# One 64 KB-row load for the first tile, weights issued after the table load, and a first token made by VectorE alone

## The chip, the core and the metric

The kernel runs on one core of one Trainium2 chip. The core has five engines with a queue of instructions each. Here three do the work: ScalarE (ACT) and VectorE (DVE) compute, SyncE (SP) only issues transfers; ACT's queue issues some transfers too. Transfers between the chip's large memory (HBM) and the on-chip memory (SBUF, 128 partitions) are carried out by 16 DMA engines, which all queues share. The metric is the device time of one execution in microseconds (us); a lower one is better.

## The reference

For each of 16 x 1024 = 16,384 tokens two expert outputs of 512 numbers are weighted and added, all in float32:

```python
batch, seq, hidden, n_experts, k = 16, 1024, 512, 8, 2
expert_outputs = randn(batch, seq, k, hidden)     # 67.1 MB
combine_weights = randn(batch, seq, k)            # 0.13 MB
out = np.sum(expert_outputs * combine_weights[..., np.newaxis], axis=2)   # 33.6 MB
```

## The kernel before, in words

**Tiles.** The 16,384 tokens are spread over 128 partitions, 128 tokens to a partition. A tile `et` holds `J` = 16 tokens of every partition: 128 rows of 16 x 1024 x 4 bytes = 64 KB, 8 MB in all. There are 8 tiles (loop on line 79, `g` = 0 to 7) and three buffers for them (`bufs=3`, line 47), so the load of tile `g` + 3 needs the store of tile `g` to be done. The text calls them load 0 to 7 and store 0 to 7.

**Weights.** All weights lie in one tile `wt`. Line 51 loads it in two transfers on ACT's queue: 112 KB (896 bytes to a partition) for tiles 0 to 6, and 16 KB (128 bytes to a partition) for tile 7.

**Warm-up.** Line 56 runs one tiny Copy on ACT, so that the loading of the function table that Copy needs comes early. In the order of ACT's queue it follows the two weight loads.

**Compute** (`combine`, lines 58 to 76). Per token ACT multiplies the first half of its 1024 numbers by the first weight, in place (line 65). DVE then computes the second half times the second weight plus ACT's result (line 68) and writes it to the front of the same tile, so a piece of `c` tokens is stored from `c` x 2 KB per partition.

**Loads and stores.** Loads are issued by SP (line 89). Tile 0 is loaded in two pieces: 2 tokens, cut into 4 KB rows by `max_dma_last_dim`, then 14 tokens in 56 KB rows; tiles 1 to 6 in one piece each with 64 KB rows; tile 7 in two pieces of 12 and 4 tokens (48 KB and 16 KB rows), each of which is computed and stored by itself. Stores of tiles 0 to 6 are issued by ACT's queue as one piece with 32 KB rows, those of tile 7 by SP in 24 KB and 8 KB rows (line 96). In the profile q1 is SP's DMA queue and q10 is ACT's: loads and the last two stores are in q1, weights and stores 0 to 6 in q10.

**What sets the order.** Each queue issues in the order of the program. SP issues loads 0, 1 and 2 at once, and each later load when the store that frees its buffer has landed. ACT issues a store when DVE has finished its tile.

Of the kernel before, what the change touches and what calls it, by code (L numbers as in the profile page):

```python
# [1 line left out]

# [4 lines left out]


@with_exitstack
def kernel(  # L10
    ctx: ExitStack,
    tc: tile.TileContext,
    expert_outputs: bass.AP,
    combine_weights: bass.AP,
    out: bass.AP,
):
    nc = tc.nc
    b, s, k, h = expert_outputs.shape
    assert k == 2
    n = b * s  # L20
    P = nc.NUM_PARTITIONS
    per = n // P
    assert per * P == n

    J = 16
    PIECES = (12, 4)
    assert sum(PIECES) == J and per % J == 0
    main = per - J
    eo = expert_outputs.rearrange("b s k h -> (b s) (k h)")
    cw = combine_weights.rearrange("b s k -> (b s) k")  # L30
    o = out.rearrange("b s h -> (b s) h")

    def rows(x):

        a = x[0 : P * main, :].rearrange("(p t) f -> p t f", p=P)
        b = x[P * main : n, :].rearrange("(p t) f -> p t f", p=P)
        return lambda t, c: a[:, t : t + c, :] if t < main else b[:, t - main : t - main + c, :]

    eo, cw, o = rows(eo), rows(cw), rows(o)

    dt = mybir.dt.float32
    mult = mybir.AluOpType.mult
    add = mybir.AluOpType.add
    copy = mybir.ActivationFunctionType.Copy

    wpool = ctx.enter_context(tc.tile_pool(name="w", bufs=1))
    ipool = ctx.enter_context(tc.tile_pool(name="in", bufs=3))

    wt = wpool.tile([P, per * k], dt)
    for t, c in ((0, main), (main, J)):  # L50
        nc.scalar.dma_start(
            out=wt[:, k * t : k * (t + c)].rearrange("p (t k) -> p t k", k=k), in_=cw(t, c)
        )

    warm = wpool.tile([P, 1], dt)
    nc.scalar.activation(out=warm, in_=nc.const_aps.tensor(1.0, (P, 1), dt), func=copy)  # L56

    def combine(et, a, c, t0):

        ot = et[:, a : a + c].rearrange("p j f -> p (j f)")[:, 0 : c * h]  # L60
        ot = ot.rearrange("p (j f) -> p j f", f=h)
        for i in range(c):
            t = t0 + a + i
            x = et[:, a + i]
            nc.scalar.activation(  # L65
                out=x[:, 0:h], in_=x[:, 0:h], func=copy, scale=wt[:, 2 * t : 2 * t + 1]
            )
            nc.vector.scalar_tensor_tensor(  # L68
                out=ot[:, i, :],
                in0=x[:, h : 2 * h],  # L70
                scalar=wt[:, 2 * t + 1 : 2 * t + 2],
                in1=x[:, 0:h],
                op0=mult,
                op1=add,
            )
        return ot

    last = per // J - 1
    for g in range(last + 1):
        et = ipool.tile([P, J, k * h], dt)  # L80
        t0 = g * J
        if g == 0:
            loads, stores = ((0, 2), (2, J - 2)), ((0, J),)
        elif g < last:
            loads = stores = ((0, J),)
        else:
            loads = stores = ((0, PIECES[0]), (PIECES[0], PIECES[1]))
        for a, c in loads:
            nc.sync.dma_start(  # L89
                out=et[:, a : a + c],  # L90
                in_=eo(t0 + a, c),
                max_dma_last_dim=k * h * 4 if t0 + a == 0 else None,
            )
        for a, c in stores:
            ot = combine(et, a, c, t0)
            (nc.sync if g == last else nc.scalar).dma_start(out=o(t0 + a, c), in_=ot)


# [1 line left out]
_INS = ['expert_outputs', 'combine_weights']  # L100
_OUTS = [((16, 1024, 512), 'float32')]


# [23 lines left out]
```

## Time and profile before

| what | value |
|---|---|
| median of 3 runs | 241.98 us (240.82 to 242.04) |
| the profiled execution | 242.21 us, of which the span from first to last instruction 240.4 us |
| busy: DVE, ACT | 87.2 us (36%), 81.0 us (34%) |
| moved by DMA | 100.82 MB, mean 419 GB/s over the span |
| one token: ACT line 65, DVE line 68 | 0.708 us, 0.746 us |
| table load, warm-up (line 56) | 1.283 us, 0.203 us |
| ACT waits for loads | 149.6 us in all, 10 times |
| SP waits for stores to free a buffer | 158.7 us in all, 5 times |

Issue and landing (the time at which the transfer's completion is seen) of some transfers, in us from the start of the span:

| transfer | issued | landed |
|---|---|---|
| tile 0, 2 tokens | 0.73 | 6.3 |
| weights, 112 KB | 0.73 | 5.4 |
| weights, 16 KB | 1.20 | 23.3 |
| tile 0, 14 tokens | 1.22 | 23.3 |
| load 1 | 1.73 | 47.72 |
| store 0 | 33.52 | 67.47 |
| load 3 | 67.55 | 106.69 |
| store 1 | 59.61 | 96.42 |
| load 7, 12 tokens | 183.86 | 217.85 |
| load 7, 4 tokens | 184.24 | 229.72 |
| store 6 | 205.62 | 226.91 |
| store 7, 12 tokens | 227.13 | 237.00 |
| store 7, 4 tokens | 233.65 | 239.42 |

How to read the profile: the page gives, among others, the busy share of the DMA engines in 40 equal slices of the span (tenths, 9 is 90% or more) and the chain of work that ended last, followed back from the last instruction. The timeline lists merged instructions with start, duration, engine, line and, in brackets, how long the engine stood idle before and for whom. The table of stretches gives for a stretch its length, the busy time of DVE, ACT and POOL, a clock, and the DMA engines' mean busy share and GB/s; packets are counted in the stretch in which they start. The DMA view gives the packets, MB and share of each queue in a window. A packet is one row of a transfer, or the 4-byte write of its completion on one of the 16 engines.

### The profile page before, as it was taken

What the parts mean: (1) busy time and instruction counts of PE and PEld (TensorE: products, weight loads), DVE (VectorE), ACT (ScalarE), POOL (GpSimd) and SP (SyncE); (2) the same over time, 40 slices, a digit from 0 to 9 for tenths busy, and PEclk for the clock granted to TensorE, in tenths of its full rate; (3) what the DMA queues carried; (4) which work ended last, traced back from release to release, by engine and by line L of the source; (5) the groups of instructions that cost most, each with busy time, mean ns of one, the idle gap of its engine ahead of it and who ended that gap; (6) DMA issues with size and microseconds to landing.
All of it is one profiled execution on the core that took longest, in us unless ns stands there. A gap on an engine that the chain in (4) does not pass through costs nothing.

```text
span 240.4 us, 412 instructions
## 1 busy us (share of the span) xinstructions
DVE 87.2 (36%) x128; ACT 81.0 (34%) x130; POOL 0.2 (0%) x4
## 2 busy tenths in 40 slices
DVE  0200950089001970019700295004930069205740
ACT  2201930095002940029400492005900078007440
POOL 0000000000000000000000000000000000000000
DMA  9989989899999999898999999999989999999895
GB/s 346 421 363 461 512 360 393 371 502 393 436 414 458 414 503 436 382 480 383 431 436 403 469 398 436 431 425 447 480 387 436 447 431 436 433 428 414 341 401 236
DMA packets 3155, 100.82 MB, mean 419 GB/s; under 512 B 464, under 2 KB 592, under 8 KB 848
## 3 DMA queue, kind: packets, MB, share of 16 engines
q1 hardware_dynamic: 1856, 71.30, 69.4%
q10 hardware_dynamic: 1296, 29.49, 28.5%
q14 instruction: 3, 0.02, 0.0%
HBM read 67.24 MB, written 33.55 MB: 419 GB/s over the span
## 4 chain that ended last, share of the span: by engine, by line
DMA 85%; DVE 6%; ACT 4%; issue 1%; SPq 1%; DVEq 0%; ACTq 0%
DMA et<-in_expert_outputs_dram 54%; DMA out_dram<-et 30%; DVE et L68 6%; ACT et L65 4%; SPq L89 1%; DVEq L122 0%; DVEq L68 0%; ACTq L65 0%
## 5 line engine op out<-in xcount | busy, mean ns | idle before, releaser
L68 DVE SCALAR_TENSOR_TENSOR et<-et,wt 128x512 f32<-128x512 f32 x128 | 87.2, 746 | 146.4 <-ACT et L65 144.6
L65 ACT ACTIVATE et<-et,wt 128x512 f32<-128x512 f32 x128 | 79.5, 708 | 149.6 <-DMA et<-in_expert_outputs_dram 149.6
L56 ACT ACT_TABLE_LOAD x1 | 1.3, 1283 | 1.7 <-issue 1.7
L56 ACT ACTIVATE warm<-const-float32-1.0 128x1 f32<-128x1 f32 x1 | 0.2, 203 | 0.0
L111 POOL MEMSET const-bfloat16-1.0<- 128x1 bf16 x1 | 0.1, 101 | 0.0
L111 POOL MEMSET const-uint8-127<- 128x1 uint8 x1 | 0.1, 101 | 0.0
L111 POOL MEMSET const-float32-0.0<- 128x1 f32 x1 | 0.1, 98 | 0.2 <-issue 0.2
L111 POOL MEMSET const-float32-1.0<- 128x1 f32 x1 | 0.1, 98 | 0.0
## 6 DMA issues: line engine op xcount, KB each, us to landing
out_dram<-et ACTq DMA_DIRECT2D x7, 4096.0 KB, 36.2
et<-in_expert_outputs_dram SPq DMA_DIRECT2D x1, 7168.0 KB, 22.1
et<-in_expert_outputs_dram SPq DMA_DIRECT2D x1, 6144.0 KB, 34.0
out_dram<-et SPq DMA_DIRECT2D x1, 3072.0 KB, 9.9
et<-in_expert_outputs_dram SPq DMA_DIRECT2D x1, 2048.0 KB, 45.5
et<-in_expert_outputs_dram SPq DMA_DIRECT2D x1, 1024.0 KB, 5.6
out_dram<-et SPq DMA_DIRECT2D x1, 1024.0 KB, 5.8
wt<-in_combine_weights_dram ACTq DMA_DIRECT2D x1, 112.0 KB, 4.6
```

Of the source, the lines that this page charges most:

```text
L56: nc.scalar.activation(out=warm, in_=nc.const_aps.tensor(1.0, (P, 1), dt), func=copy)
L65: nc.scalar.activation(out=x[:, 0:h], in_=x[:, 0:h], func=copy, scale=wt[:, 2 * t : 2 * t + 1])
L68: nc.vector.scalar_tensor_tensor(out=ot[:, i, :], in0=x[:, h : 2 * h], scalar=wt[:, 2 * t + 1 : 2 * t + 2], in1=x[:, 0:h], op0=mult, op1=add,)
L89: nc.sync.dma_start(out=et[:, a : a + c], in_=eo(t0 + a, c), max_dma_last_dim=k * h * 4 if t0 + a == 0 else None,)
L111: nc = _bacc.Bacc("TRN2", target_bir_lowering=False, num_devices=1)
```

## The change

Three things are changed. The order on ACT's queue: the warm-up, and with it the table load, goes first, and `issue_after` keeps the two weight loads behind it in the queue's order (an order within one engine, without a semaphore). The first token of every piece: DVE makes both products, the first with an added `tensor_scalar`, and ACT starts with the second token; a piece is 16 tokens, and 12 and 4 in tile 7. The loads: tile 0 comes in one transfer of 16 tokens in 64 KB rows like the others; tile 7 is as it was.

```diff
     wt = wpool.tile([P, per * k], dt)
-    for t, c in ((0, main), (main, J)):
-        nc.scalar.dma_start(
-            out=wt[:, k * t : k * (t + c)].rearrange("p (t k) -> p t k", k=k), in_=cw(t, c)
-        )
-
     warm = wpool.tile([P, 1], dt)
-    nc.scalar.activation(out=warm, in_=nc.const_aps.tensor(1.0, (P, 1), dt), func=copy)
+    table = nc.scalar.activation(out=warm, in_=nc.const_aps.tensor(1.0, (P, 1), dt), func=copy)
+    with tc.issue_after(table.ins):
+        for t, c in ((0, main), (main, J)):
+            nc.scalar.dma_start(
+                out=wt[:, k * t : k * (t + c)].rearrange("p (t k) -> p t k", k=k), in_=cw(t, c)
+            )
...
-            nc.scalar.activation(
-                out=x[:, 0:h], in_=x[:, 0:h], func=copy, scale=wt[:, 2 * t : 2 * t + 1]
-            )
+            w0 = wt[:, 2 * t : 2 * t + 1]
+            if i == 0:
+
+                nc.vector.tensor_scalar(
+                    out=x[:, 0:h], in0=x[:, 0:h], scalar1=w0, scalar2=None, op0=mult
+                )
+            else:
+                nc.scalar.activation(out=x[:, 0:h], in_=x[:, 0:h], func=copy, scale=w0)
...
-        if g == 0:
-            loads, stores = ((0, 2), (2, J - 2)), ((0, J),)
-        elif g < last:
-            loads = stores = ((0, J),)
-        else:
-            loads = stores = ((0, PIECES[0]), (PIECES[0], PIECES[1]))
-        for a, c in loads:
-            nc.sync.dma_start(
-                out=et[:, a : a + c],
-                in_=eo(t0 + a, c),
-                max_dma_last_dim=k * h * 4 if t0 + a == 0 else None,
-            )
-        for a, c in stores:
+        pieces = ((0, J),) if g < last else ((0, PIECES[0]), (PIECES[0], PIECES[1]))
+        for a, c in pieces:
+            nc.sync.dma_start(out=et[:, a : a + c], in_=eo(t0 + a, c))
+        for a, c in pieces:
             ot = combine(et, a, c, t0)
```

## The prediction

> **What bounds the kernel now.** I read the chain of waits first, then the DMA line of the page, then the same stretch by stretch.
>
> ```profile
> DMA  9989989899999999898999999999989999999895
> DMA 85%; DVE 6%; ACT 4%; issue 1%; SPq 1%; DVEq 0%; ACTq 0%
> wt<-in_combine_weights_dram ACTq DMA_DIRECT2D x1, 112.0 KB, 4.6
> ```
> ```profile
> 60.00:220.00 160.00, 55.55 (x82) 51.62 (x84) 0.00 (x0) 1.00 1.00 433
> 226.00:228.00 2.00, 1.10 (x2) 0.00 (x0) 0.00 (x0) 1.00 0.37 156
> ```
>
> The chain is nearly all transfers. In the table of stretches (the last two figures are DMA share and GB/s) the 16 DMA engines are full for 160 us at 433 GB/s. So the span is a start of some 1.9 us, 100.82 MB / 433 = 232.8 us, an end of 1.4 us (last packet to last instruction), and 4.3 us lost elsewhere. Only those 4.3 can be won. The clear hole is 226 to 228 us: 2 x (1 - 0.37) = 1.26 us. The timeline shows what is awaited there:
>
> ```profile
> 217.93 7.46 ACT L65 ACTIVATE et<-et,wt 128x512 f32<-128x512 f32 x12 [14.25 <-DMA et<-in_expert_outputs_dram]
> 218.68 8.43 DVE L68 SCALAR_TENSOR_TENSOR et<-et,wt 128x512 f32<-128x512 f32 x12 [13.09 <-ACT et L65]
> 227.13 6.86 SPq L96 DMA_DIRECT2D out_dram<-et  x2
> ```
>
> Loads and earlier stores have run dry, and the store of the 12-token piece is issued only at 227.13.
>
> How the two queues share the engines decides the rest. These are the DMA view's queue lines (packets, MB, share) in three windows: 9.0 to 11.12 us, 96.2 to 125.2 us, and 37 to 39.5 us (its q10 line).
>
> ```profile
> q1 hardware_dynamic: 16, 0.92, 99.8%
> q10 hardware_dynamic: 16, 0.00, 0.6%
> ```
> ```profile
> q1 hardware_dynamic: 143, 8.32, 66.3%
> q10 hardware_dynamic: 143, 4.19, 33.5%
> ```
> ```profile
> q10 hardware_dynamic: 4, 0.13, 12.1%
> ```
>
> In 2.12 us each engine takes one 56 KB row of loads (q1) and one 128-byte packet of weights (q10); later, 143 against 143. **A turn is one row, whatever its size, and the queues alternate.** A transfer has 8 rows and a completion on each engine, so 9 turns. At 433 GB/s a 64 KB row lasts 16 x 65,536 / 433 = 2.42 us, 48 KB 1.82, 32 KB 1.21, 24 KB 0.91, 16 KB 0.61. The third window shows that store 0 began on 4 engines one load row before the other 12 (which follow at 39.9 to 40.4). From there on these four are behind in loads; the 12-token piece is complete on twelve engines by 215 us, on the last at 217.4.
>
> **Head: one load in 64 KB rows.** It removes an issue of SP (0.46 us, off the path), 256 packets of 4 KB and 128 of 56 KB, and adds 128 of 64 KB: the same bytes. Up to 5.1 us 1.04 MB moved; from the first packet at 1.8 us the full rate would have moved 1.43. So 0.39 MB, 0.9 us, was lost to start-up and small packets. What of it is start-up, and stays, no row shows: the gain is 0 to 0.9, I take the middle, 0.45. Tokens 0 and 1, made during the load (6.41 to 8.77), now come after it: 2 x 0.69 = 1.4 us on the store of tile 0.
>
> **Weights behind the table load.** ACT's queue issued both weight loads at 0.73 to 1.70, then the table load (1.28) and the warm-up (0.20). Now these two come first and the weights are issued between 0.75 (if the queue runs ahead of its engine) and 2.25; I take the later. Their first packets came 1.6 us after issue, so at 3.9. They no longer meet 4 KB packets but 64 KB rows, from 1.9 us on. They follow row 1 at the earliest; I take row 2, because store 0, issued at 33.52, still let 12 engines start a load row at 36.6 to 37.2, as if one row is picked ahead. Then the 8th packet falls after tile 0's completion and the completion after the first row of tile 1: 1.9 + 0.5 for start-up (an estimate, about half of the 0.9 above) + 0.3 for its own packets (8 x 0.04) + 9 x 2.42 = 24.5, landed about 25.0, where tile 0 lands at about 22.6. That is **a new wait of 2.4 us** (0 if they follow row 1, 4.8 with one turn more lost). Behind it stand all of tile 0's ACT and DVE work, and store 0 on ACT's queue: 25.0 + (59.61 - 47.72 = 11.9, landing to issue for 16 tokens) = 36.9 instead of 33.52. The second weight load (16 KB) is ahead of store 0 in q10 and has 9 turns too, against tile 1's rows: store 0's first row goes only after the second row of tile 2, at 2.7 + 18 x 2.42 = 46.3 (before: 37.4 to 40). So the late compute is covered by some 8 us; without that cover it would still only let loads go first.
>
> The Trainium skill, DMA: Bandwidth & Descriptors, section Queues, rings and completion order, says an engine changes queue after a packet of about 9 to 17 descriptors. By that rule all 8 weight rows go in one turn, the weights land near 7 us, nothing waits, and store 0 is issued near 34.5; the windows above show one row per turn, so the trace decides against it.
>
> **What is late next: load 3**, which reuses tile 0's buffer. Loads of tiles 0 to 2 have 27 turns; store 0 takes 9, from t2's row 2, so it ends with load 2: 46.3 + 6 x 2.42 + 8 x 1.21 = 70.5, landed 71 (before 67.47). q1 is then empty until load 3's first row: 0.45 landing, 0.1 SP, 0.85 to 1.6 to first packet. The engines stay full, because store 1 is issued at 41.9 + 11.9 = 53.8; it gets b = 3 rows alone. From here q10 has 54 turns, 3 of them gone, and q1 has 45 up to the end of the 12-token piece. Counting one against one, 10 - b = 7 q10 turns are left then (6 rows and a completion). Before it was 7 on twelve engines, 6 on four.
>
> **Tail.** With 7 left on every engine, 6 x 1.21 + 8 x 0.61 = 12.1 us of transfers lie after that piece. The path to its store is 0.45 landing + 9.28 (217.85 to 227.13) + 0.85 (227.13 to the first packet) = 10.6. The hole is covered by 1.5 us: gain **1.26**, and the last piece's work (3.9 us) lies under 8 x 0.91 = 7.3 us of that store.
>
> **First token by VectorE.** Not in the trace: a tensor_scalar of 128x512. Bounds: 0.10 (POOL's memset of 128x1) and 0.746 (line 68, same shape, one source more). It is nearest to the latter, spaced at 0.69. It replaces ACT's 0.75 ahead of DVE: 0.06 a piece (0 to 0.65), and nothing where the hole is closed. The Trainium skill, VectorE: DVE Perf Modes, section on the perf-mode tier table, gives such an fp32 operation double rate; by it some 0.33 us, a gain of 0.4 where the hole stays open. No row here shows it.
>
> **Sum.** 242.21 (the profiled execution, 0.23 above the median) - 0.45 - 1.26 = 240.5; I say 240.4 for the 0.06s.
>
> **Rivals.**
> *The hole stays* (0.33). Engines differ by up to 0.8 us in phase, and load 3 arrives while 1.21 us rows run. If some engines let it in a row earlier than others, the laggards again set the landing. Against it: at store 0 the rows were twice as long, and it needed a skew there too. Or the one engine that ended at 238.99, the others at 237.9, gains nothing. 242.21 - 0.45 - 0.06 = 241.7: no change.
> *Load 3 comes back late* (0.15, slower). Place: q1 between store 0's end and load 3's first row. Each row of store 1 that passes (1.21 us) takes a row from the tail's cover: b = 4 leaves 0.3 us, b = 5 a hole of 0.9, b = 6 of 2.1 (242.6), b = 7 of 3.3: 242.21 - 0.45 + 2.05 = 243.8. It is slower by over 0.5% from b = 7, 8.5 us without loads. For it: store 0 took 3.8 us from issue to first packet; the same here makes 4.35 us in all, b = 4, or 5 on an engine that is 0.8 us ahead. Against: more than that is nowhere seen.
> *The hole closes and more* (part of the first case): all 0.9 of the head and one engine's lag of 1.1: 239.3.
>
> **Numbers.** Forecast 0.52. About 0.5% (1.2 us) is what a measurement here can tell from no change. The forecast's own range, 239.3 to 241.3, lies across that bound (240.77), so 0.44 of it and a little besides counts as faster: faster 0.45, same 0.40 (mostly the second case), slower 0.15. Range 239.3 to 242.8: from the full head gain to b = 6.
>
> **What would show it.** Right: the first 112 KB of weights lands near 25 us and ACT waits for it, not for tile 0; store 0 issued near 37 but landed near 71; load 3 issued right after; the DMA share of the 2 us ahead of the 12-token piece's store near 1. Wrong: weights landing with 4.6 us again; a stretch between 60 and 75 us with share under 0.95; a load 3 whose first rows come after 76 us; the hole before the last stores as wide as 1.3 us.

## The result, and the profile after

| | before | changed kernel |
|---|---|---|
| median | 241.98 us (240.82 to 242.33) | 249.59 us (249.28 to 250.08) |
| ratio, 95% interval | | 1.0325 (1.0296 to 1.0354) |
| profiled execution, span | 242.21 us, 240.4 us | 249.43 us, 247.6 us |

The change costs 3.2%. The prediction was a small gain, 240.4 us with a range of 239.3 to 242.8: it was wrong, in its sign too. Of the page of the changed kernel these are the DMA engines' busy tenths, the chain by engine, the group of the added instruction (busy time and mean ns of one after the bar), and the two weight transfers with their us to landing. Line 68 is now the `tensor_scalar`, line 73 the `scalar_tensor_tensor`, line 72 ACT's Copy, line 92 the stores:

```profile
DMA  9999998989979999898999999989989999995087
DMA 82%; DVE 7%; ACT 4%; issue 2%; SPq 0%; DVEq 0%; ACTq 0%
L68 DVE TENSOR_SCALAR et<-et,wt 128x512 f32<-128x512 f32 x9 | 4.4, 487 | 145.0 <-DMA et<-in_expert_outputs_dram 121.6
wt<-in_combine_weights_dram ACTq DMA_DIRECT2D x1, 112.0 KB, 22.5
wt<-in_combine_weights_dram ACTq DMA_DIRECT2D x1, 16.0 KB, 41.5
```

The busy row ends in "5087" where before it ended in "9895": one whole slice of 6.2 us near the end is empty. The table of stretches (DMA share and GB/s last) narrows it down:

```profile
70.00:76.00 6.00, 3.99 (x7) 4.23 (x7) 0.00 (x0) 1.00 1.07 437
76.00:80.00 4.00, 4.00 (x8) 4.00 (x8) 0.00 (x0) 1.00 0.87 270
80.00:220.00 140.00, 50.77 (x77) 40.70 (x66) 0.00 (x0) 1.00 1.00 432
226.00:228.00 2.00, 0.00 (x0) 0.00 (x0) 0.00 (x0) 1.00 0.41 172
228.00:236.00 8.00, 7.67 (x12) 1.95 (x3) 0.00 (x0) 1.00 0.00 1
```

The hole of 1.26 us, which the prediction expected to close, has become about 9.5: 1.2 in the first of the last two rows, all 8 of the second, 0.3 more until the first packet of the next store. The timeline of the same stretch shows why:

```profile
217.54 0.49 DVE L68 TENSOR_SCALAR et<-et,wt 128x512 f32<-128x512 f32 x1 [11.38 <-DMA et<-in_expert_outputs_dram]
217.55 6.85 ACT L72 ACTIVATE et<-et,wt 128x512 f32<-128x512 f32 x11 [13.68 <-DMA et<-in_expert_outputs_dram]
218.06 1.61 DVE L73 SCALAR_TENSOR_TENSOR et<-et,wt 128x512 f32<-128x512 f32 x2
228.33 1.95 ACT L72 ACTIVATE et<-et,wt 128x512 f32<-128x512 f32 x3 [3.94 <-DMA et<-in_expert_outputs_dram]
228.33 0.48 DVE L68 TENSOR_SCALAR et<-et,wt 128x512 f32<-128x512 f32 x1 [8.66 <-DMA et<-in_expert_outputs_dram]
228.74 9.74 DVE L73 SCALAR_TENSOR_TENSOR et<-et,wt 128x512 f32<-128x512 f32 x14
235.47 3.38 SPq L92 DMA_DIRECT2D out_dram<-et  x2
```

The 12-token piece landed at 217.44, as early as before. ACT went through its eleven tokens without a stop. VectorE did two `scalar_tensor_tensor` of the twelve and then stood still for 8.66 us: the next instruction in its queue was the `tensor_scalar` of the **4-token piece**, which waits for a load that lands at 228.31. Ten instructions of the 12-token piece, all of them with their inputs ready by 224.4, stood behind it. So the store that was issued at 227.13 before goes at 235.47, 8.34 us later, and nothing is left for the DMA engines to do meanwhile. The end moved by less, 7.2 us, because in the profile of before one DMA engine finished 1.1 us behind the others and set the end; here all finish within 0.2.

VectorE's lines above stand in the order in which they ran: a `tensor_scalar` and two `scalar_tensor_tensor` of the 12-token piece, the `tensor_scalar` of the 4-token piece, then fourteen `scalar_tensor_tensor`, ten of the one piece and four of the other. This is not the order of the source, which has all of the 12-token piece first; it was set when the program was compiled, for an edge in the program changes it (next section). Before, VectorE ran one kind of instruction, each of which waited for ACT, in source order.

### The profile page after: what moved, and what is told of

Its sections match the earlier page's. It is cut to its first block, busy times and chain, and to the rows that moved or that the text cites. A ratio compares the mean times of both kernels' runs of the same rounds, so it can differ in the third digit from the quotient of the medians.

```text
span 247.6 us, 408 instructions
## 1 busy us (share of the span) xinstructions
DVE 91.4 (37%) x137; ACT 75.4 (30%) x121; POOL 0.2 (0%) x4
## 4 chain that ended last, share of the span: by engine, by line
DMA 82%; DVE 7%; ACT 4%; issue 2%; SPq 0%; DVEq 0%; ACTq 0%
DMA et<-in_expert_outputs_dram 52%; DMA out_dram<-et 30%; DVE et L73 7%; ACT et L72 4%; SPq L89 0%; DVEq L118 0%; DVEq L73 0%; DVE et L68 0%; ACTq L72 0%
## 5 line engine op out<-in xcount | busy, mean ns | idle before, releaser
L72 ACT ACTIVATE et<-et,wt 128x512 f32<-128x512 f32 x119 | 73.9, 708 | 154.2 <-DMA et<-in_expert_outputs_dram 133.0
L68 DVE TENSOR_SCALAR et<-et,wt 128x512 f32<-128x512 f32 x9 | 4.4, 487 | 145.0 <-DMA et<-in_expert_outputs_dram 121.6
## 6 DMA issues: line engine op xcount, KB each, us to landing
wt<-in_combine_weights_dram ACTq DMA_DIRECT2D x1, 16.0 KB, 41.5
```

What stands on the lines that cost most here:

```text
L68: nc.vector.tensor_scalar(out=x[:, 0:h], in0=x[:, 0:h], scalar1=w0, scalar2=None, op0=mult)
L72: nc.scalar.activation(out=x[:, 0:h], in_=x[:, 0:h], func=copy, scale=w0)
```

## The experiments

The kernel before was run again beside each group of experiments, with medians of 241.47 to 241.65 us; the ratios are to those.

**Which part of the change costs the time.** First the changed kernel with one edge added: a piece's `tensor_scalar` may not go ahead of the last `scalar_tensor_tensor` of the piece traced before it.

```diff
             if i == 0:
+                with tc.issue_after(prev[-1].ins) if prev else nullcontext():
                     nc.vector.tensor_scalar(...)
...
+        prev.append(made)      # the piece's last scalar_tensor_tensor
```

> The changed kernel, but every tensor_scalar is kept behind the last scalar_tensor_tensor of the piece before it on VectorE's queue. Theory (VectorE stands still behind the last piece's tensor_scalar, which sits ahead of ten instructions of the 12-token piece): the 12-token store is issued near 226.4 us (217.5 + 0.5 + 12 x 0.69) instead of 235.5, and the time falls by 9.0 to about 240.5. Rival (the late weights and the later load 3 cost the time): nothing of that is touched, so at least 247.

Measured: 242.11 us, ratio to before 1.002 (1.000 to 1.004). The end of its timeline (its lines 69 and 74 are the changed kernel's 68 and 73, 95 is the store):

```profile
219.66 0.49 DVE L69 TENSOR_SCALAR et<-et,wt 128x512 f32<-128x512 f32 x1 [12.59 <-DMA et<-in_expert_outputs_dram]
220.19 8.42 DVE L74 SCALAR_TENSOR_TENSOR et<-et,wt 128x512 f32<-128x512 f32 x12
228.64 5.84 SPq L95 DMA_DIRECT2D out_dram<-et  x2
```

All twelve run through, and the store goes 9.1 us after the piece landed (219.57) instead of 18.0. One edge brings the ratio from 1.0325 down to 1.002, nearly all of the loss. It does not reach the 240.5 that was expected; the part on the head, below, tells why (with the 16 KB of weights moved as well the same kernel takes 240.70).

Then the kernel before with VectorE's token and nothing else.

```diff
+            if i == 0:
+                nc.vector.tensor_scalar(
+                    out=x[:, 0:h], in0=x[:, 0:h], scalar1=w0, scalar2=None, op0=mult
+                )
+            else:
                 nc.scalar.activation(out=x[:, 0:h], in_=x[:, 0:h], func=copy, scale=w0)
```

> The kernel before with the first token of each piece made by VectorE, and nothing else of the change. Theory: the last piece's tensor_scalar is again ahead of ten instructions of the 12-token piece and waits for a load that lands near 229.7, so its store is issued near 229.7 + 0.5 + 10 x 0.69 = 237.1 instead of 227.1, and the time is 250 to 252. Rival (loads and weights are the cause): 241.5 to 242, or a little less.

Measured: 249.42 us, ratio 1.0335 (1.0308 to 1.0362). Its load and weights are those of before, and it is as slow as the whole change. It is a little below the expected 250; the last piece landed at 228.1 here, not at the 229.7 that the expectation went by:

```profile
217.72 1.61 DVE L72 SCALAR_TENSOR_TENSOR et<-et,wt 128x512 f32<-128x512 f32 x2
228.12 0.48 DVE L67 TENSOR_SCALAR et<-et,wt 128x512 f32<-128x512 f32 x1 [8.79 <-DMA et<-in_expert_outputs_dram]
235.25 3.38 SPq L100 DMA_DIRECT2D out_dram<-et  x2
```

Next the rest without the token: the changed kernel with ACT making every token.

```diff
-            if i == 0:
+            if False:
```

> The changed kernel with ACT making every token as before: the new load and the weights behind the table load alone. Theory: 12-token store issued near 217.5 + 9.3 = 226.8, about 240.9 (240.3 to 242). Rival (loads and weights are the cause): 247 to 250.

Measured: 241.78 us, ratio 1.0006 (0.999 to 1.002), within what was expected of the theory. The new load and the place of the weights, together, are worth nothing that can be measured.

**Is it the wait, or what stands behind it?** The last piece's `tensor_scalar` is put between the eighth and the ninth `scalar_tensor_tensor` of the 12-token piece, with an edge on either side (shortened).

```diff
+            at8 = c == PIECES[0] and i == 8
+            if at8:
+                with tc.issue_after(made.ins):
+                    early = nc.vector.tensor_scalar(...)     # first token of the 4-token piece
...
+            if at8: stack.enter_context(tc.issue_after(early.ins))
             made = nc.vector.scalar_tensor_tensor(
```

> The changed kernel with the last piece's tensor_scalar put behind eight of the twelve instructions of the 12-token piece instead of two. Theory: the same wait to about 228.3, but only four instructions (2.8 us) stand behind it instead of ten (6.9): the store is issued near 231.6, 3.9 earlier, and the time is about 245.6, between the changed kernel and the one with the order kept. Rival: no change, 249.6.

Measured: 246.59 us, ratio 1.0209 (1.0186 to 1.0233).

```profile
217.84 5.78 DVE L85 SCALAR_TENSOR_TENSOR et<-et,wt 128x512 f32<-128x512 f32 x8
229.10 1.95 ACT L72 ACTIVATE et<-et,wt 128x512 f32<-128x512 f32 x3 [4.92 <-DMA et<-in_expert_outputs_dram]
229.10 0.49 DVE L78 TENSOR_SCALAR et<-et,wt 128x512 f32<-128x512 f32 x1 [5.49 <-DMA et<-in_expert_outputs_dram]
232.26 3.38 SPq L105 DMA_DIRECT2D out_dram<-et  x2
```

From the start of the instruction that waited for the load to the store it is now 232.26 - 229.10 = 3.16 us with four instructions behind the wait, against 235.47 - 228.33 = 7.14 with ten: 4.0 for six, 0.66 each, which is their spacing of 0.69. The time came out 1 us above the expectation; this run's last piece landed 0.8 later than the expectation took it. So the store goes when the late load has landed and the work queued behind the instruction that waits for it is done. The standstill is the same delay counted from the front: it is 8.66 us in the changed kernel and 5.49 here, and from the landing of their piece to their store the two take 9.0 and 6.0 us longer than the kernel with the order kept (18.0 and 15.0 against 9.1).

**The head.** The kernel before with the weights behind the table load alone:

```diff
+    with tc.issue_after(table.ins):
         for t, c in ((0, main), (main, J)):
             nc.scalar.dma_start(
```

> The kernel before with the weights behind the table load, and nothing else of the change. Theory: the queue issues them without waiting for the engine (0.79 us in the changed kernel's trace, beside 0.73), so the 112 KB land near 5.4 us again and the time is that of before, 241.7. Rival (my prediction's choice, issue only after the warm-up at 2.25 us): landing 7 us or later, and still before 23, so the time is the same: the landing tells them apart.

Measured: 241.51 us, ratio 0.9999 (0.998 to 1.002). From its page:

```profile
wt<-in_combine_weights_dram ACTq DMA_DIRECT2D x1, 112.0 KB, 4.6
```

The same 4.6 us as before. The changed kernel's timeline shows the same: ACT's queue issues the weights at 0.79, while its engine is still loading the table and before the warm-up that stands ahead of them.

```profile
0.72 1.28 ACT L51 ACT_TABLE_LOAD   x1 [0.72 <-PEq L107]
0.79 0.87 ACTq L54 DMA_DIRECT2D wt<-in_combine_weights_dram  x2
2.01 0.20 ACT L51 ACTIVATE warm<-const-float32-1.0 128x1 f32<-128x1 f32 x1
```

This part of the change moves a transfer by 0.06 us, which is nothing. Then the single load alone, with the weights issued first as before:

```diff
-        if g == 0:
-            loads, stores = ((0, 2), (2, J - 2)), ((0, J),)
-        elif g < last:
+        if g < last:
...
-                max_dma_last_dim=k * h * 4 if t0 + a == 0 else None,
+                max_dma_last_dim=None,
```

> The kernel before with tile 0 in one load of 64 KB rows, weights issued first as before, ACT making every token. Theory (a turn is one row): the 112 KB of weights land near 23 us with tile 0, although issued first, the 16 KB near 42.5 with tile 1; store 0's first row goes near 44 us and its landing near 72 leaves the load queue empty for about five store rows. What the start gains is lost there: 241.8 as with the whole head. Rival: weights issued first slip in ahead of the rows and land near 5 us, store 0 lands near 67.5.

Measured: 242.10 us, ratio 1.002 (1.000 to 1.004). Its page:

```profile
wt<-in_combine_weights_dram ACTq DMA_DIRECT2D x1, 112.0 KB, 22.5
wt<-in_combine_weights_dram ACTq DMA_DIRECT2D x1, 16.0 KB, 41.5
```

So it is the rows of 64 KB beside them that make the weights late: they land at 23.2 with tile 0 (23.05) and 42.6 with tile 1 (42.5). Store 0, issued at 35.1, stands behind the second weight transfer and has its first rows at 44.2. To see whether this holds the gain back, the 16 KB were moved behind store 0, with ACT making every token (shortened):

```diff
     with tc.issue_after(table.ins):
+        weights(0, main)
...
+            if g == 0:
+                with tc.issue_after(st.ins):      # st: store 0
+                    weights(main, J)
```

> The changed kernel with ACT making every token and the 16 KB of weights issued behind store 0 instead of ahead of it. Theory (store 0 goes late because the 16 KB transfer has nine turns ahead of it in its queue): store 0, issued near 34.9, has its first rows near 39 instead of 44 and lands near 67; load 3 is issued near 67 and its queue does not run empty, so the stretch at 312 GB/s near 76 to 80 us is gone. The engines then lose about 1.2 us at store 0's first rows, as the kernel before does: 241.3 to 242. Rival (the 64 KB rows or the late 112 KB hold store 0 back): first rows still near 44, slow stretch still there.

Measured: 240.79 us, ratio 0.9969 (0.9951 to 0.9987), **0.3% faster than before**, and better than expected; against the same kernel with the 16 KB ahead of store 0 (1.0006) the intervals do not meet. The queues between 70.6 and 76.6 us (packets, MB, share), the changed kernel and then this one:

```profile
q10 hardware_dynamic: 95, 2.59, 105.8%
q1 hardware_dynamic: 16, 0.00, 0.1%
```
```profile
q1 hardware_dynamic: 61, 2.95, 113.5%
q10 hardware_dynamic: 82, 0.17, 7.3%
```

In the changed kernel the load queue has only 16 completions there, one for each engine, and not one row, while the store queue moves 95 - 16 = 79 rows, five on an engine: load 3, issued at 72.01, comes back after five rows of store 1. With the 16 KB behind store 0, load 3 is issued at 67.25 and loads flow on. What each choice loses can be worked out from the packet records: a stretch's length less the bytes moved in it at 434.2 GB/s (16 rows of 64 KB in the usual 2.42 us are 433.7), each packet spread evenly over its duration, in us. Each row is one execution:

```
                        0-6   6-70  70-100  100-225  225-end
before                  2.80  1.29   0.05    0.15     3.94
before, weights behind  2.76  0.81   0.05    0.19     3.19
changed                 2.66  0.32   1.41    0.15    10.91
ACT makes every token   2.60  0.33   1.45    0.16     2.97
16 KB behind store 0    2.61  0.90   0.09    0.25     2.95
```

The first two rows are practically one kernel, profiled at 242.21 and at 240.99 us: in the second and the last stretch they differ by 0.5 and 0.75, so a difference of that size between two rows says nothing of a change. The new load gains 0.1 to 0.2 at the start. The transition from loads alone to loads and stores costs 0.8 to 1.3 before; with the weights ahead of store 0 it costs 0.3, but 1.4 is lost when load 3 comes back. This last loss is firm: from 70 to 100 us the six traces with 64 KB rows for tile 0 and the 16 KB ahead of store 0 lose 1.4 to 1.6, the seven others 0.05 to 0.10. Putting the 16 KB behind store 0 loses the least of these five in sum, but only 0.2 less than the second row.

Where the 1.4 goes can be seen row by row. In the changed kernel 17 rows of loads that start between 76.6 and 82.3 us took 2.96 to 3.76 us instead of 2.42, and 14 rows of store 1 just ahead of them 1.32 to 1.94 instead of 1.21. Together that is 1.36 us on an engine.

**Attempts on the hole and on the rest.** The kernel before with tile 7 in three pieces:

```diff
-    PIECES = (12, 4)
+    PIECES = (6, 6, 4)
```

> The kernel before with tile 7 in pieces of 6, 6 and 4 tokens instead of 12 and 4. Theory (the hole ahead of the last stores is 1.26 us of the 16 engines waiting for 12 tokens' work): the first store is issued about 4 us earlier, the hole is gone, 240.4 (239.8 to 241). Rival (the end is set by one lagging DMA engine, or the hole only moves): 241.5 to 242.

Measured: 241.72 us, ratio 1.0004 (0.999 to 1.002): no gain, as the rival had it. In the profiled execution, a faster one (241.11), the hole is gone, and half of the DMA engines have done their work by 236.1 (the median of their last completions), but two end at 238.0. That such laggards take the gain in the other executions too is not shown.

The same pieces in the changed kernel with the order kept:

> The changed kernel with the order on VectorE's queue kept and tile 7 in pieces of 6, 6 and 4. Theory: the hole is gone here too, 240.5; VectorE's token adds nothing to that. Rival: as with 12 and 4 tokens, 242.1.

Measured: 241.87 us, ratio 1.0015 (1.000 to 1.003): nothing again. Last, the whole change with both mends, the order kept and the 16 KB behind store 0, and the same with `PIECES = (11, 5)`:

> The whole change with two mends: the order on VectorE's queue kept, and the 16 KB of weights behind store 0. Theory: both costs of the change are gone; VectorE's own token brings the 12-token store 0.26 us forward, and the hole ahead of it in the run without that token was about 0.7 us of the engines, so 240.5 (240.0 to 241.0), ahead of the kernel before (241.6) and of 240.79. Rival (the token costs something beside the order): 241 or more.

> The same with tile 7 in 11 and 5 tokens. Theory (the rest of the hole is the 12-token piece's compute): the first store comes 0.7 us earlier relative to its load, and that load is a twelfth shorter; the hole closes, 240.2. Rival (the lag of single DMA engines sets the end, as with 6, 6 and 4): no gain, 240.5 to 241.2.

Measured: 240.70 us, ratio 0.9967 (0.995 to 0.999), and 240.68 us, ratio 0.9966 (0.995 to 0.998). Both beat the kernel before, and neither stands clear of the 240.79 without VectorE's token (0.9969). VectorE's token is harmless once its order is kept, and worth nothing that can be seen; 11 and 5 tokens instead of 12 and 4 are worth nothing either. The medians of the mended kernels are only some 0.1 us below the fastest executions of the kernel before, which took 240.8 to 240.9; what they lack is its spread, which reaches 242.9. With both mends eleven of twelve executions lie between 240.63 and 240.78, the twelfth at 242.26. What makes an execution of the kernel before slow stayed open.

## Why the prediction was wrong, point by point

**The step that failed** is the tail: "The path to its store is 0.45 landing + 9.28 (217.85 to 227.13) + 0.85", together with "It replaces ACT's 0.75 ahead of DVE: 0.06 a piece". Both priced the added instruction by its duration and took VectorE's queue in the order of the source. It was not asked what would stand behind the wait that the change adds. Before, VectorE waited for ACT alone; the `tensor_scalar` waits for a load directly, and for the last piece that load lands 10.9 us after the one before it. With the compiled order the step reads: the late landing 228.31 + 0.5 + 10 x 0.69 = 235.7 for the store, measured 235.47; that is 18.0 us after its piece landed, where the prediction had 9.28. That this order is the cause is shown by taking it away (242.11), by bringing it alone (249.42) and by halving what stands behind it (246.59). Why the instruction was placed after two of the twelve stayed open.

**The rival on the slow side** had the wrong mechanism. Load 3 did come back late, with b = 5 rows instead of the 3 that were taken, and by the prediction's count that leaves a hole of 0.9 us in the tail. The whole head, with that late load, measured 1.0006. The count did not hold to the end either: in the run where ACT makes every token, each engine still had six 32 KB rows behind the 12-token piece, as twelve of them had before. The stores came too late there to take every turn: store 3 was issued at 119.30, 12.0 us after load 3 had landed, and from 119.4 to 121.8 us the load queue started a row on each of the 16 engines, while the store queue started one row and the last 15 completions of store 2. So loads got turns alone again.

**A turn is one row**: right, and it carried the head. The first weights landed at 23.3 beside tile 0, and store 0 was held up behind the second weights, at 44.0 where 46.3 was said. The missing 2.3 us are one turn: the weights follow the first row of the load, with first packets at 4.79, where the prediction took the second. It had also taken the later of two issue times, 0.75 and 2.25, and it was 0.79; no run tells whether that made the turn. By the same turn the "new wait of 2.4 us" was 0.2 (23.30 against 23.13), and store 0 was issued at 35.03 instead of 36.9, still covered by the 9 us that it stood in its queue.

**The head's gain** was mis-sized: 0.45 was taken, 0.1 to 0.2 measured. Most of the 0.9 that was lost there is start-up and stays: 15 of the 16 first rows of 64 KB took 2.88 to 3.35 us instead of 2.42, which is 0.7 us on an engine. The late load 3 had a price that the sum did not hold: 1.4 us, although the engines were never without work, for some rows took longer. Its first rows came at 76.6, and "first rows come after 76 us" was one of the prediction's own signs of being wrong. So even without the error in the tail there was no gain: 241.78.

**VectorE's token** lasted 0.487 us, not 0.69. The Trainium skill, VectorE: DVE Perf Modes, section on the perf-mode tier table, was right that such an operation runs faster than one with two tensor sources (here 0.746, a `scalar_tensor_tensor`, for which the table has no row). In the trace the factor is 1.5, and the estimate of 0.33 made from that page was too low.

## What to carry to other kernels

An instruction that a change gives to another engine takes its wait along: ask what it waits for, which other work is queued behind it in the *compiled* order, and when the thing it waits for arrives. Two pieces that share an engine and have loads far apart needed an explicit order between them here. And here a small transfer on a second queue took as many turns on each engine as it had rows there, each behind a row of the other queue: put such a transfer where nothing urgent follows it.

## What the runs showed that was not expected

- ACT's queue issued DMAs at 0.79 us while the table load of the instruction ahead of them ran from 0.72 to 2.00.
- A transfer of 16 KB, queued behind one of 112 KB, took 41.5 us to land beside 64 KB rows. It was 22.1 where the 112 KB ahead of it, beside 4 KB rows, took 4.6 and it met 56 KB rows itself.
- When loads came back beside running stores, the full DMA engines moved less: 1.4 us lost, with none of them idle, because about one row of loads and one of stores on each engine took longer. The same happened when stores first joined the loads (28 rows of loads from 35.0 to 41.5 us took 2.5 to 3.9 in the kernel before). What causes it stayed open.
- In several profiles one or two DMA engines finished about 1 to 2 us behind the others, and they set the end; which and why stayed open.
